# Folded query weights: their seven-product sums made in the fold, and the fold's stores on ScalarE's queue

## The chip, the cores and the metric

The kernel runs on one core of a Trainium2 chip. The core has a matrix engine (TensorE, PE in the profile), a vector engine (VectorE, DVE), an activation engine (ScalarE, ACT), a general engine (GpSimd, POOL) and a synchronisation engine (SyncE, SP). Each takes its own list of instructions in order and waits on semaphores that the others raise. Transfers are issued by SP, POOL or ACT and are carried by 16 DMA engines which all of them share. The metric is the time of one execution in device microseconds. Here the median before the change is 2603.19 us of three runs (2600.45 to 2605.1).

## The reference: what is computed

One layer over 2048 tokens of width 1024, all in float32, with three sub-layers. Each is an RMS norm, a body, an RMS norm of the output and a residual sum.

```python
y = jnp.concatenate([ya, yh], axis=-1) @ w_out       # window attention and gated recurrence, one out projection
h = h + rms_norm(y, g_mix_post)
u = rms_norm(h, g_x_pre);  m = rms_norm(mem, g_mem)
y = cross_attention(u, m, wq_x, wk_x, wv_x, wo_x)     # 4 heads of 256 over 256 memory tokens
h = h + rms_norm(y, g_x_post)
u = rms_norm(h, g_ffn_pre)
y = (silu(u @ w_gate) * (u @ w_up)) @ w_down          # hidden width 2816
h = h + rms_norm(y, g_ffn_post)
```

In cross-attention the memory is short (256 tokens), so the kernel multiplies weights with the memory first. The scores are `u @ QK`, where `QK` (1024 x 1024) is, head by head, the query weight times the keys, with the gain and the scale in it. The output is `p @ VO`, where `VO` (1024 x 1024) is the values times the output weight. Making `QK` and `VO` is called the fold.

## The kernel before

**Number format.** A float32 matrix is split into a high and a low half (`split2`, L893: ACT or POOL makes the high one, DVE the low one), and each product is three TensorE passes (L1032 to L1034: high x high, high x low, low x high).

**Seven products.** The large products from the out projection on are done in a Strassen-Winograd scheme: both operands are cut in two by two blocks and seven block products stand for eight (`seven`, L1036). It needs sums of blocks on both sides. On the streamed side (`streamed`, L974) DVE makes them for each block of 256 rows (L1001). On the side that stays in SBUF (`resident`, L903, tiles `T`) four sums are needed, named by keys 5, 7, 6 and 4 (`CHAIN`, L901). With the four blocks of the matrix called 11, 12 (upper left and right), 21 and 22 (lower), they are 5 = 12 - 11, 7 = 22 - 12, 6 = 7 + 11 and 4 = 21 - 6. They are made ahead of their use and written to a buffer in HBM, from which `resident` loads them.

**Who makes the sums ahead.** `combined` (L936) is a generator that runs beside an earlier stage. For each half of the matrix it loads blocks, waits a few steps, lets DVE subtract or add (L943, placed behind the last traced ACT and DVE instructions by `behind`) and stores the result (L944). In one pass it loads six tiles of 512 KB and stores four, for two halves twelve and eight. `jobs` (L1291) names the stage beside which each set is made: the sums of `QK` (`qk_s`) beside the out projection from its third block on, and those of `VO` (`vo_s`) beside the score product.

**The order of the stages around the change.** The recurrence of the second half of the tokens (`hgrn`, L856) and the fold (`fold_cross`, L277) are interleaved step by step: recurrence and key projection, then the eight 128-column groups of the query weight (L309 to L322), then the value projection, then the four heads of the output weight (L325 to L348). Both the query weight's groups and the output weight's heads end in an ACT eviction from PSUM into a row tile named `x` (three buffers of 512 KB) and a store from there: 128 rows of `QK` to `qk_d` at L321, or 128 rows of `VO` to `vo_d` at L347. All these stores are issued by SP, which also issues every load. After the fold the SBUF pools are closed and those of the streamed stages are opened. The first stage there is the out projection (`mixed_block`, L1400), with `T` from `w_s` and the stream `sraw` from `y_d`. Its evictions add on DVE (L1391). Then the rows are normed and scaled (L1417), the residual is added by a transfer that POOL issues (L1398, `row<-in_x_dram`), the rows are stored and transposed on PE (L1284, evicted at L1285), and the transposed rows are stored for the score product (`score_block`, L1434).

**What sets the order.** Each engine's list is written by a planner that runs over the traced program with its own costs. Within an engine nothing overtakes at run time: an instruction that waits holds all behind it.

Of the kernel before, what the change touches and what calls it, by code (L numbers as in the profile page):

```python
# [11 lines left out]
F32 = mybir.dt.float32  # L12
# [3 lines left out]
ALU = mybir.AluOpType  # L16
AX = mybir.AxisListType

P = 128
T = 2048  # L20
D = 1024
# [3 lines left out]
KT = D // P  # L25
# [4 lines left out]
NT = T // P  # L30
# [6 lines left out]
def f32(ap):  # L37
    return ap.bitcast(F32)
# [10 lines left out]
class Layer:  # L49
# [26 lines left out]

    def store(self, dst, src):
        self.nc.sync.dma_start(dst, src)

    def gain_tile(self):  # L80
        self._n += 1
        return self.gp.tile([P, D], F32, tag="g", name=f"g_{self._n}")
# [46 lines left out]
    def raw_tile(self):  # L129
        self._n += 1  # L130
        return self.wp.tile([P, D], F32, tag="raw", name=f"raw_{self._n}", bufs=3)

    def split_tiles(self):
        self._n += 1
        hi = self.wp.tile([P, D], F32R, tag="hi", name=f"whi_{self._n}", bufs=3)
        lo = self.wp.tile([P, D], F32R, tag="lo", name=f"wlo_{self._n}", bufs=3)
        return hi, lo
# [139 lines left out]
    def fold_cross(self):  # L277

        nc, ph = self.nc, self.xp
        gx = ph.tile([P, KT], F32, name="gx")  # L280
        self.load(gx, self.I["g_x_pre"].rearrange("r (k p) -> p (r k)", p=P))
        nc.vector.tensor_scalar_mul(gx, gx, float(M) ** -0.5)
        g = self.gain(self.I["g_mem"])
        mT = [ph.tile([P, KT, M], F32R, name=f"mT{i}") for i in range(2)]
        raw_tile, split_tiles = self.raw_tile, self.split_tiles

        def projected(w):
            dst = [ph.tile([P, KT, M], F32R, tag=f"kv{i}", name=f"kv{i}_{self._n}") for i in range(2)]
            for j in range(KT):
                wh, wl = self.wcols(w, j, "A")  # L290
                ps = self.bank("sh"[j % 2])[:, :M]
                for part in range(2):
                    if part:
                        yield dst
                    self.mm3(ps, [((wh[:, k, :], wl[:, k, :]), (mT[0][:, k, :], mT[1][:, k, :])) for k in range(KT)],
                             part)
                nc.scalar.activation(dst[0][:, j, :], ps, AF.Copy)
                nc.vector.tensor_tensor(dst[1][:, j, :], ps, f32(dst[0][:, j, :]), ALU.subtract)
                yield dst

        for t in range(M // P):
            m = raw_tile()
            self.load(m, self.I["mem"][t * P:(t + 1) * P, :])
            u = self.pre_norm(m, g)
            self.transpose_split(u, lambda q: mT[0][:, 4 * q:4 * q + 4, t * P:(t + 1) * P],
                                 lambda q: mT[1][:, 4 * q:4 * q + 4, t * P:(t + 1) * P])
        for kT in projected(self.I["wk_x"]):
            yield
        for d in range(KT):  # L309
            th, tl = self.wcols(self.I["wq_x"], d, "A")  # L310
            o = self.io_tile("x")
            for q in range(2):
                ps = self.bank("sh"[q])
                for r in range(2):
                    h = 2 * q + r
                    self.mm3(ps[:, r * M:(r + 1) * M],
                             [((th[:, j, :], tl[:, j, :]), (kT[0][:, j, :], kT[1][:, j, :])) for j in (2 * h, 2 * h + 1)])
                sl = slice(q * 512, (q + 1) * 512)
                nc.scalar.activation(o[:, sl], ps, AF.Copy, scale=gx[:, d:d + 1])
                if q:  # L320
                    self.store(self.qk_d[d * P:(d + 1) * P, :], o)  # L321
                yield  # L322
        for vT in projected(self.I["wv_x"]):
            yield
        for h in range(4):  # L325
            banks = [[self.bank(k) for k in "sh"] for _ in range(2)]
            for i in range(2):
                j = 2 * h + i
                raw = raw_tile()
                self.load(raw, self.I["wo_x"][j * P:(j + 1) * P, :])  # L330
                wh, wl = split_tiles()
                self.split(raw, wh, wl, "A")
                for mt in range(2):
                    ms = slice(mt * P, (mt + 1) * P)
                    ah, al = vT[0][:, j, ms], vT[1][:, j, ms]
                    for q in range(2):
                        sl = slice(q * 512, (q + 1) * 512)
                        nc.tensor.matmul(banks[mt][q], ah, wh[:, sl], start=(i == 0), stop=False)
                        nc.tensor.matmul(banks[mt][q], ah, wl[:, sl], start=False, stop=False)
                        nc.tensor.matmul(banks[mt][q], al, wh[:, sl], start=False, stop=(i == 1))  # L340
                if i == 0:
                    yield
            for mt in range(2):
                o = self.io_tile("x")
                for q in range(2):
                    nc.scalar.activation(o[:, q * 512:(q + 1) * 512], banks[mt][q], AF.Copy)
                self.store(self.vo_d[(2 * h + mt) * P:(2 * h + mt + 1) * P, :], o)  # L347
            yield  # L348


# [585 lines left out]
    def combined(self, get, nk, dst):  # L936

        nc = self.nc
        halves = [(0, (nk + 1) // 2), ((nk + 1) // 2, nk)]
        for a, b in halves:  # L940
            def put(key, t, o, op):
                with self.behind():
                    nc.vector.tensor_tensor(t, t, o, op)  # L943
                self.store(dst[self.CHAIN.index(key), :, a * 512:b * 512], t.rearrange("p k d -> p (k d)"))  # L944

            for x, y, key in (((0, 1), (0, 0), 5), ((1, 1), (0, 1), 7), (None, (0, 0), 6), (None, (1, 0), 4)):
                if x:
                    t = get(0, *x, a, b - a)
                o = get(1, *y, a, b - a)
                for _ in range(3):  # L950
                    yield
                if key == 4:
                    put(4, o, t, ALU.subtract)
                else:
                    put(key, t, o, ALU.add if key == 6 else ALU.subtract)
                yield

    @contextlib.contextmanager
# [117 lines left out]
    def eight(self, S, T, nk, out, addend, halves=False):  # L1076
# [34 lines left out]
        yield  # L1111

    def phases(self, jobs, first, prologue=None):


# [175 lines left out]
    def jobs(self):  # L1291
# [11 lines left out]
        def weights(src, r0, nk):  # L1303
            return lambda t, i, j, k0, n: self.load(
                t, src[r0 + (i * nk + k0) * P:r0 + (i * nk + k0 + n) * P, j * 512:(j + 1) * 512]
                .rearrange("(k p) d -> p k d", p=P))

        def ffn_u(b):
            return lambda t, i, j, k0, n: self.load(
                t, self.u_d[4 * i + k0:4 * i + k0 + n, :, b * TB + j * 512:b * TB + (j + 1) * 512]  # L1310
                .rearrange("k p t -> p k t"))

        def kinds(blocks, first="dd", last="dd"):
            middle = "s" * (len(blocks) - len(first) - len(last))
            return [(k,) + b for k, b in zip(first + middle + last, blocks)]

        def sums(name, src, nk, *tiles):
            dst = self.tc.dram_tile([4, P, nk * 512], F32, name=name)

            def get(which, i, j, k0, n):  # L1320
                t = (tiles or (self.extra_tile, self.gain_tile))[which]().rearrange("p (k d) -> p k d", d=512)[:, :n]
                src(t, i, j, k0, n)
                return t

            return dst, lambda: self.combined(get, nk, dst)

        def in_turn(*what):
            return lambda: itertools.chain.from_iterable(w() for w in what)

        qk, vo = weights(self.qk_d, 0, 4), weights(self.vo_d, 0, 4)  # L1330
        down = [(weights(I["w_down"], f0 * P, nk), f0, nk) for f0, nk in ((0, 3), (6, 4), (14, 4))]
        qk_s, vo_s = sums("qk_s", qk, 4, self.extra_tile, self.row_tile), sums("vo_s", vo, 4)
        u_s = sums("u_s", ffn_u(1), 4)
        x_tile = lambda: self.io_tile("x")
        w_s, self.w_sums = sums("w_s", w_out, 4, x_tile, x_tile)
        self.u_s = self.tc.dram_tile([4, P, 4, 512], F32, name="u_s0")
        d_s = [sums(f"d_s{c}", src, nk) for c, (src, _, nk) in enumerate(down)]
        jobs = [(w_out, 4, kinds([self.mixed_block(n) for n in range(0, NT, 2)]), w_s, {2: [qk_s[1]]}),
                (qk, 4, kinds([self.score_block(n) for n in range(0, NT, 2)]), qk_s[0], {1: [vo_s[1]]}),
                (vo, 4, kinds([self.value_block(n) for n in range(0, NT, 2)]), vo_s[0], {})]  # L1340
        for b in range(NB):
            beside = {2: [in_turn(*(d[1] for d in d_s))]} if b else {4: [u_s[1]]}
# [323 lines left out]
```

## Time and profile before

| | |
|---|---|
| median of three runs | 2603.19 us |
| the profiled execution | 2603.6 us |
| its span, first to last instruction | 2601.7 us |
| mean granted TensorE clock | 0.992 |
| PE / DVE / ACT / POOL busy | 97% / 67% / 49% / 18% |
| moved by DMA | 497.88 MB, mean 191 GB/s |
| recurrence with fold | about 655 to 791 us |
| out projection, and its overlap with the score product | about 797 to 1000 us |

Times in rows are microseconds from the span's start. A row of the timeline has the start, the duration, the engine, the line, the operation with output and inputs, the shape, and in brackets how long the engine had been idle and what ended that. `xN` at the end of a row counts merged instructions; the duration of a merged row runs to the end of its last one. A row of the windows has the stretch, its length, then for PE, weight load (PEld), DVE, ACT and POOL the busy time with the number of instructions, then the granted TensorE clock, the DMA engines' busy share and GB/s. A row by tile has minimum, median and maximum in nanoseconds. `SPq` and the like is an engine's own issue of a transfer.

### The profile page before, as it was taken

To read this page: it belongs to the slowest core of one execution; us is meant where nothing else is said; L and a number is where in the kernel's file an instruction comes from. 1 tells how busy PE (TensorE), PEld (TensorE's weight loads), DVE (VectorE), ACT (ScalarE), POOL (GpSimd) and SP (SyncE) were. 2 spreads that over 40 slices of the span, in tenths; PEclk is the share of its full clock that TensorE was granted. 3 is DMA by queue.
4 is the path that set the end of the run, shared out by engine and by line. 5 is a ranking of instruction groups with operands and counts; after the bars stand their busy time and mean duration, and the time that the engine had idled before them with its cause. 6 is when DMAs were issued, how large, how long until landed. Compare 5 with 4: busy or idle time off the path is not lost.

```text
span 2601.7 us, 34516 instructions
## 1 busy us (share of the span) xinstructions
PE 2528.0 (97%) x12160; PEld 2115.2 (81%) x12160; DVE 1746.0 (67%) x2773; ACT 1262.0 (49%) x2641; POOL 466.6 (18%) x651
## 2 busy tenths in 40 slices
PE   7989999999998999999999999999999999999998
PEld 6878788878997778888778888888888888888786
DVE  7675578887646568786785555576666656664756
ACT  5463366655654565565563333354333335443543
POOL 4240343320312224223320000000000000000022
PEclk9999999999999999999999999999999999999999
DMA  5434655484875998656984532353456434576798
GB/s 186 143 120 167 208 157 171 131 267 157 279 259 207 289 328 258 221 191 187 302 273 138 167 124 73 105 186 116 167 182 230 147 108 168 174 225 174 232 228 208
DMA packets 286350, 497.88 MB, mean 191 GB/s; under 512 B 20576, under 2 KB 143456, under 8 KB 286176
## 3 DMA queue, kind: packets, MB, share of 16 engines
q1 hardware_dynamic: 275520, 456.87, 52.3%
q0 software_dynamic: 10656, 38.80, 8.0%
q8 instruction: 96, 1.57, 0.2%
q14 instruction: 78, 0.64, 0.1%
HBM read 328.87 MB, written 166.72 MB: 190 GB/s over the span
## 4 chain that ended last, share of the span: by engine, by line
PE 80%; DMA 8%; DVE 4%; issue 3%; POOL 2%; ACT 2%; SPq 0%; DVEq 0%; POOLq 0%; ACTq 0%
PE psm L1032 22%; PE psm L1034 22%; PE psm L1033 22%; PE psg L163 2%; PE psg L164 2%; PE psg L165 2%; DMA row<-in_x_dram 1%; PE pss L1284 1%; DMA row<-h_d 1%; DMA u_d<-row 1%; DMA h_d<-row 1%; DMA x<-in_w_out_dram 1%; ACT junk L1369 1%; DMA pair<-in_x_dram 1%; DMA extra<-qk_d 0%
## 5 line engine op out<-in xcount | busy, mean ns | idle before, releaser
L1032 PE MATMUL psm<-T,S 128*128 128x512 f32 x2664 | 1036.4, 393 | 24.6 <-ACT S L896 13.8
L1033 PE MATMUL psm<-T,S 128*128 128x512 f32 x2664 | 1041.9, 391 | 0.0
L1034 PE MATMUL psm<-T,S 128*128 128x512 f32 x2664 | 1037.3, 392 | 2.6 <-DVE S L899 2.5
L1032 PEld LDWEIGHTS psm<-T,S 128*128 128x128 f32 x2664 | 503.3, 189 | 132.6 <-ACT S L896 15.1
L1034 PEld LDWEIGHTS psm<-T,S 128*128 128x128 f32 x2664 | 502.5, 189 | 109.2 <-DVE S L899 4.8
L1033 PEld LDWEIGHTS psm<-T,S 128*128 128x128 f32 x2664 | 503.2, 189 | 103.3
L896 ACT ACTIVATE S<-sum 128x512 fp32r<-128x512 f32 (+1 forms) x338 | 208.0, 619 | 340.1 <-PE psm L1034 331.7
L899 DVE TENSOR_TENSOR S<-sraw,S 128x512 fp32r<-128x512 f32 (+1 forms) x311 | 214.4, 697 | 224.4 <-ACT S L896 214.9
L899 DVE TENSOR_TENSOR S<-sum,S 128x512 fp32r<-128x512 f32 (+1 forms) x404 | 277.1, 690 | 84.3 <-ACT S L896 66.6
L1047 ACT ACTIVATE part<-psm 128x512 f32<-128x512 f32 x297 | 175.1, 592 | 174.9 <-PE psm L1034 168.0
L896 ACT ACTIVATE S<-sraw 128x512 fp32r<-128x512 f32 (+1 forms) x272 | 166.8, 617 | 154.7 <-PE psm L1034 143.1
L1398 POOL DMA_DIRECT2D row<-y_d x28 | 25.0, 892 | 1131.4 <-DMA sraw<-hid_d 964.8
L1369 ACT ACTIVATE junk<-row 128x512 f32<-128x512 f32 x160 | 99.7, 624 | 121.8 <-DVE row L1391 33.4
L899 DVE TENSOR_TENSOR T<-row,T 128x1024 fp32r<-128x1024 f32 x104 | 123.0, 1190 | 28.7 <-ACT T L896 28.5
L163 PE MATMUL psg<-u,whi 128*128 128x512 f32 x352 | 141.2, 401 | 1.0 <-POOL whi L145 1.0
L165 PE MATMUL psg<-u,wlo 128*128 128x512 f32 x352 | 139.5, 396 | 1.5 <-DVE wlo L146 1.5
L164 PE MATMUL psg<-u,whi 128*128 128x512 f32 x352 | 139.6, 397 | 0.0
L896 ACT ACTIVATE T<-row 128x1024 fp32r<-128x1024 f32 x104 | 105.8, 1027 | 23.7 <-DMA row<-in_w_down_dram 10.9
L146 DVE TENSOR_TENSOR wlo<-raw,whi 128x1024 fp32r<-128x1024 f32 x54 | 68.8, 1275 | 33.2 <-ACT whi L143 26.6
L898 POOL TENSOR_SCALAR S<-sum 128x512 fp32r<-128x512 f32 x66 | 49.0, 742 | 234.7 <-PE psm L1034 141.0
L1550 DVE TENSOR_TENSOR part<-psm,part 128x512 f32<-128x512 f32 x66 | 45.4, 688 | 64.6 <-PE psm L1034 64.5
L1541 DVE TENSOR_TENSOR row<-psm,part 128x512 f32<-128x512 f32 x66 | 45.5, 689 | 57.4 <-PE psm L1034 57.3
(329 smaller groups left out, 3644.3 us busy)
## 6 DMA issues: line engine op xcount, KB each, us to landing
sraw<-in_w_gate_dram SPq DMA_DIRECT2D x44, 512.0 KB, 4.9
sraw<-in_w_up_dram SPq DMA_DIRECT2D x44, 512.0 KB, 4.8
hid_d<-row SPq DMA_DIRECT2D x44, 512.0 KB, 2.7
h_d<-row SPq DMA_DIRECT2D x32, 512.0 KB, 6.9
y_d<-row SPq DMA_DIRECT2D x32, 512.0 KB, 3.6
sraw<-hid_d SPq DMA_DIRECT2D x32, 512.0 KB, 5.2
row<-h_d POOLq DMA_DIRECT2D x30, 512.0 KB, 8.1
row<-y_d POOLq DMA_DIRECT2D x28, 512.0 KB, 7.3
```

The lines of the kernel that those rows point to most:

```text
L146: nc.vector.tensor_tensor(lo, raw, f32(hi), ALU.subtract)
L163: nc.tensor.matmul(ps, ah, bh, start=(i == 0), stop=False)
L164: nc.tensor.matmul(ps, ah, bl, start=False, stop=False)
L165: nc.tensor.matmul(ps, al, bh, start=False, stop=(i == n - 1))
L896: self.nc.scalar.activation(hi, raw, AF.Copy)
L898: self.nc.gpsimd.tensor_scalar(hi, raw, 1.0, 1.0, ALU.mult, ALU.mult)
L899: self.nc.vector.tensor_tensor(lo, raw, f32(hi), ALU.subtract)
L1032: nc.tensor.matmul(ps, s[:, 0, k, :], t[:, 0, k, :], start=st, stop=False, **kw)
L1033: nc.tensor.matmul(ps, s[:, 0, k, :], t[:, 1, k, :], start=False, stop=False, **kw)
L1034: nc.tensor.matmul(ps, s[:, 1, k, :], t[:, 0, k, :], start=False, stop=sp, **kw)
L1047: nc.scalar.activation(t, ps, AF.Copy)
L1369: self.nc.scalar.activation(junk, a, AF.Square, scale=float(D) ** -0.5, accum_out=to)
```

## The change

Three things change.

1. The column groups of the query weight are taken in the order 0, 4, 1, 5, 2, 6, 3, 7. The row tile of an upper group (0 to 3) is kept until that of the lower group four further on is there. From the two, DVE makes the four sums of `CHAIN` for these rows: `a` is 5 (left) and 7 (right), `b` is 6 (left) and 4 (right). Two row tiles `qs` of 512 KB are added for them. SP stores the four halves of 256 KB each to `qk_s`, for four pairs of groups: 16 sums of 128x512 and 16 stores.
2. The pass of `combined` over `QK` beside the out projection is gone, with its twelve loads, eight sums of 128x1024 and eight stores. `qk_s` is now a buffer that only the fold writes.
3. The fold's 16 stores of `x` rows, eight to `qk_d` and eight to `vo_d`, are issued by ACT instead of SP.

```diff
+    def put(self, dst, src):
+        self.nc.scalar.dma_start(dst, src)
...
-        for d in range(KT):
+        upper = None
+        for d in (0, 4, 1, 5, 2, 6, 3, 7):
             th, tl = self.wcols(self.I["wq_x"], d, "A")
             o = self.io_tile("x")
...
                 nc.scalar.activation(o[:, sl], ps, AF.Copy, scale=gx[:, d:d + 1])
                 if q:
-                    self.store(self.qk_d[d * P:(d + 1) * P, :], o)
+                    self.put(self.qk_d[d * P:(d + 1) * P, :], o)
                 yield
+            if d < 4:
+                upper = o
+                continue
+            a, b = [ph.tile([P, D], F32, tag="qs", name=f"qs{d}_{i}", bufs=2) for i in range(2)]
+            l, r = slice(0, 512), slice(512, D)
+            nc.vector.tensor_tensor(a[:, l], upper[:, r], upper[:, l], ALU.subtract)
+            nc.vector.tensor_tensor(a[:, r], o[:, r], upper[:, r], ALU.subtract)
+            nc.vector.tensor_tensor(b[:, l], a[:, r], upper[:, l], ALU.add)
+            nc.vector.tensor_tensor(b[:, r], o[:, l], b[:, l], ALU.subtract)
+            for c, t in enumerate((a[:, l], a[:, r], b[:, l], b[:, r])):
+                self.store(self.qk_s[c, :, (d - 4) * 512:(d - 3) * 512], t)
...
-                self.store(self.vo_d[(2 * h + mt) * P:(2 * h + mt + 1) * P, :], o)
+                self.put(self.vo_d[(2 * h + mt) * P:(2 * h + mt + 1) * P, :], o)
...
-        qk_s, vo_s = sums("qk_s", qk, 4, self.extra_tile, self.row_tile), sums("vo_s", vo, 4)
+        self.qk_s = self.tc.dram_tile([4, P, 4 * 512], F32, name="qk_s")
+        vo_s = sums("vo_s", vo, 4)
...
-        jobs = [(w_out, 4, kinds([self.mixed_block(n) for n in range(0, NT, 2)]), w_s, {2: [qk_s[1]]}),
-                (qk, 4, kinds([self.score_block(n) for n in range(0, NT, 2)]), qk_s[0], {1: [vo_s[1]]}),
+        jobs = [(w_out, 4, kinds([self.mixed_block(n) for n in range(0, NT, 2)]), w_s, {}),
+                (qk, 4, kinds([self.score_block(n) for n in range(0, NT, 2)]), self.qk_s, {1: [vo_s[1]]}),
```

The helper inside `combined` is renamed from `put` to `made`, since `put` is now a method; it does the same.

More of the change, by code (lines that the diff above doesn't have):

```diff
@@ L940, in combined, with made @@
         for a, b in halves:
-            def put(key, t, o, op):
+            def made(key, t, o, op):
                 with self.behind():
@@ L952, in combined @@
                 if key == 4:
-                    put(4, o, t, ALU.subtract)
+                    made(4, o, t, ALU.subtract)
                 else:
-                    put(key, t, o, ALU.add if key == 6 else ALU.subtract)
+                    made(key, t, o, ALU.add if key == 6 else ALU.subtract)
                 yield
```

## The prediction

> **What bounds the kernel now.** I read the page's busy shares and chain first, then the engine windows, then what TensorE (PE) waited for between 640 and 1000 us, where all edited code runs, and last the timelines around each of those waits. Lines 1 and 2 are of the page; then waits as total, times, longest; then windows.
>
> ```profile
> PE 2528.0 (97%) x12160; PEld 2115.2 (81%) x12160; DVE 1746.0 (67%) x2773; ACT 1262.0 (49%) x2641; POOL 466.6 (18%) x651
> PE 80%; DMA 8%; DVE 4%; issue 3%; POOL 2%; ACT 2%; SPq 0%; DVEq 0%; POOLq 0%; ACTq 0%
> ...
> PE psm L1032 <- ACT S L896: 6.9, 1, 6.9
> PE pss L1284 <- DMA row<-in_x_dram: 5.3, 2, 2.9
> PE pss L1284 <- ACT row L1285: 2.3, 2, 2.0
> PE psm L1032 <- DVE row L1391: 1.4, 1, 1.4
> PE psm L1032 <- ACT part L1047: 0.8, 1, 0.8
> ...
> 690.00:760.00 70.00, 68.65 (x580) 68.30 (x579) 34.05 (x46) 39.98 (x104) 23.20 (x27) 1.00 0.81 268
> 760.00:790.00 30.00, 30.00 (x165) 25.69 (x164) 12.37 (x13) 17.00 (x27) 0.00 (x0) 1.00 0.66 232
> 850.00:950.00 100.00, 92.19 (x425) 75.41 (x424) 56.57 (x73) 50.93 (x125) 30.27 (x53) 0.97 0.95 297
> 1000.00:1100.00 100.00, 100.00 (x483) 83.21 (x482) 80.04 (x148) 57.46 (x147) 27.12 (x37) 0.99 0.72 240
> ```
>
> PE is busy 97% of the span, so no edit beside it pays unless it touches one of PE's few gaps. The change removes no matmul. Three stretches matter: the fold (690 to 790: PE full, DMA 0.81 then 0.66), the out projection (850 to 950: PE loses 7.8 us while DMA is at 0.95) and, to compare, the score stage (PE full at DMA 0.72).
>
> **Part 1, the fold's stores leave SP's queue.** The timeline at the border between fold and out projection:
>
> ```profile
> 775.46 1.77 SPq L75 DMA_DIRECT2D raw<-in_wo_x_dram  x2
> 790.18 0.39 PE L340 MATMUL psh<-whi,kv 128*128 128x512 f32 x1
> 790.37 0.32 SPq L78 DMA_DIRECT2D vo_d<-x  x1
> 790.71 0.62 ACT L346 ACTIVATE x<-psh 128x512 f32<-128x512 f32 x1
> 790.78 1.25 SPq L75 DMA_DIRECT2D sraw<-y_d  x2
> 796.82 0.63 ACT L896 ACTIVATE S<-sraw 128x512 fp32r<-128x512 f32 x1 [5.50 <-DMA sraw<-y_d]
> 797.50 0.79 PE L1032 MATMUL psm<-T,S 128*128 128x512 f32 x1 [6.94 <-ACT S L896]
> ...
> 757.51 0.75 DVE L852 SCALAR_TENSOR_TENSOR sg<-psg,onorm,sg 128x512 f32<-128x512 f32 x1 [1.34 <-DMA sg<-z_d]
> ...
> 798.00:800.00 2.00, 2.00 (x6) 1.47 (x5) 0.87 (x2) 0.63 (x1) 0.00 (x0) 0.50 1.05 410
> 800.00:802.00 2.00, 2.00 (x8) 1.57 (x7) 1.25 (x2) 0.63 (x1) 0.47 (x1) 0.72 1.05 406
> ```
>
> The first stream load (`sraw<-y_d`) is issued at 790.78 because SP takes its queue in order and a `vo_d` store, which waits for ACT's eviction, stands ahead of it until 790.37. Its data come 6.0 us later, after PE has run dry at 790.57. The memory it fills was the recurrence's, whose last DVE instruction starts at 757.51, so nothing else holds it. With the stores on ACT's queue SP is done with the fold at 777.2 and the load can land before 785. Next in line is then ACT: its last eviction ends at 791.33, the cast takes 0.63, PE starts at about 792.0. The gap falls from 6.94 to 1.4: -5.5. PE also restarted at half clock (0.50, then 0.72: half until 801.1), 3.6 us at half is 1.8 lost; after a gap of 1.39 us (below, at 910) I take none. Sum -7.3. Ends: 0 (the loads come as late as now) and -8.7 (no gap left).
>
> ACT now issues 16 stores. No row shows ACT issuing one: below, SP needs 0.33 for such a store, POOL 0.89 for its kind. I take SP's, the same sort of plain transfer: 16 x 0.33 = 5.3 us of ACT, up to 14.3. ACT is idle 30.0 of 70 us in the first stretch and 13.0 of 30 in the second, so the price is 0; uncovered it would be those 5.3. A gain below zero is excluded for ACT's own time. What queues behind a store on ACT is the next weight cast (L143) and eviction. SP loses 16 stores and gets 16 others.
>
> **Part 2, no sums beside the out projection.** The loads, sums and stores around the three largest gaps of 850 to 950:
>
> ```profile
> 869.17 1.23 DVE L943 TENSOR_TENSOR extra<-extra,row 128x1024 f32<-128x1024 f32 x1 [3.52 <-DMA row<-qk_d]
> 871.51 2.47 DVE L1417 SCALAR_TENSOR_TENSOR row<-row,q_r,g 128x1024 f32<-128x1024 f32 x2
> 873.09 0.94 POOL L1398 DMA_DIRECT2D row<-in_x_dram  x1 [4.51 <-DVE row L1417]
> 882.40 1.34 PE L1284 MATMUL pss<-ident,row 128*128 128x128 f32 x8 [2.40 <-DMA row<-in_x_dram]
> 908.23 1.23 DVE L943 TENSOR_TENSOR extra<-extra,row 128x1024 f32<-128x1024 f32 x1 [5.51 <-DMA extra<-qk_d]
> 910.21 0.47 PE L1032 MATMUL psm<-T,S 128*128 128x512 f32 x1 [1.39 <-DVE row L1391]
> 919.34 0.95 POOL L1398 DMA_DIRECT2D row<-in_x_dram  x1 [1.68 <-DVE row L1417]
> 930.10 1.26 PE L1284 MATMUL pss<-ident,row 128*128 128x128 f32 x8 [2.94 <-DMA row<-in_x_dram]
> ...
> 884.00:886.00 2.00, 2.00 (x6) 1.61 (x5) 0.69 (x1) 1.28 (x4) 0.46 (x1) 0.50 1.02 353
> 886.00:888.00 2.00, 2.00 (x9) 1.57 (x9) 1.81 (x3) 1.50 (x6) 1.10 (x3) 0.89 1.02 418
> 932.00:934.00 2.00, 2.00 (x6) 1.60 (x5) 2.00 (x4) 1.10 (x4) 0.00 (x0) 0.50 0.58 232
> ```
>
> The edit takes out 12 loads and 8 stores of 512 KB (10.5 MB) and 8 sums at 1.2 us. The gap of 882 begins with the sum: DVE sits 3.52 us at L943 for a sum's load, so the scaling (L1417) and POOL's adding transfer are late. That of 910 is the same wait, 5.51 long, with the eviction L1391 behind it. That of 930 is the adding transfer itself, 10.8 us from issue to use while DMA is full. Of the 29.7 MB that 850 to 950 moves (297 GB/s) up to 10.5 go, which brings the DMA share to 0.95 x 19.2 / 29.7 = 0.61, below the 0.72 at which the score stage runs PE full. So I take all four gaps: 2.40 + 1.39 + 2.94 + 0.8 = 7.5. After 882 and 930 PE ran 3.4 us at half clock (the 0.50 rows and their neighbours), 1.7 lost each. Sum -10.9. Ends: -5.5 (882 with its clock and 910 only, where the removed wait itself is the cause) and -14.6 (also the 2.0 gap at 999 with 1.7 of clock, which hangs on a store under a full DMA). The freed DVE and SP time is worth nothing more.
>
> [...]
>
> **Part 3, sums in the fold.** Added are 16 sums of 128x512 and 16 stores of 256 KB (4.2 MB). Rows for their prices, from the fold's transfers and the groups by tile:
>
> ```profile
> q1 hardware_dynamic: 14935, 18.62, 80.7%
> qk_d<-x SPq DMA_DIRECT2D x8, 512.0 KB, 5.2
> L78 SPq DMA_DIRECT2D qk_d<-x x8: 319/332/506, 704.9 to 745.7; - x8
> L1398 POOL DMA_DIRECT2D row<-y_d x28 | 25.0, 892 | 1131.4 <-DMA sraw<-hid_d 964.8
> L1001 DVE TENSOR_TENSOR sum<-sraw,sraw x4: 678/693/954, 800.8 to 823.4; 128x512 f32<-128x512 f32 x4
> 719.24 0.69 DVE L823 TENSOR_TENSOR W<-psg,W 128x512 f32<-128x512 f32 x1 [2.88 <-PE psg L821]
> 735.76 0.69 DVE L843 TENSOR_TENSOR on<-pst,h_rs 128x512 f32<-128x512 f32 x1 [2.87 <-POOL h_rs L842]
> ```
>
> DVE: 16 x 0.69 = 11.1 us, beside 36 us of idle DVE in 690 to 760. Each pair is a chain of 2.8 us waiting for ACT's second eviction; behind it stand the next low halves (L146) and the recurrence. DVE has holes of 2.9 us just there, so 0; uncovered, 2.8 per pair or 11.1. SP: 16 x 0.33 = 5.3 us of issue, each behind a sum, ahead of weight and recurrence loads. DMA: 80.7% of 70 us for 18.62 MB is 3.03 us per MB, so 4.2 MB need 12.7 us of all engines; 13.3 are free in 690 to 760, but the stores fall in its last 45 us, where about 8.6 are free. 4.1 us are over and delay loads: +4.1. Ends: 0 (the rest spills past 760, where 10.2 are free) and +12.7 (all on the path). The new order of columns and the longer life of `x` rows cost nothing by themselves: a row is freed one column later, and columns are 5.8 us apart (8 stores from 704.9 to 745.7) against a 2.8 us chain.
>
> **Sum.** -7.3 - 10.9 + 4.1 = -14.1. The profiled execution took 2603.6 us (span 2601.7), the median is 2603.19, so nearly the same. 2603.6 - 14.1 = 2589.5 is the forecast.
>
> **Rivals.** *The border stays (R1).* The loads are late for another reason, such as transfers that share the same engines. For it: DMA reads 1.05 at 798. Against: DMA is at 0.66 before 790 and SP's wait is plain. Only part 1 drops: 2603.6 - 10.9 + 4.1 = 2596.8. [...]
>
> *The fold pays in full (R2).* DMA is the bound there: +12.7, and the stores it delays take half of part 1: 2603.6 - 3.7 - 10.9 + 12.7 = 2601.7, no change. For it: 0.81 and a PE that has used 68.65 of 70 us. Against: nobody waits soon for these stores.
>
> *ACT is held by its own stores (R3, slower).* If a store on ACT blocks it until an earlier transfer lands (5.2 us median), 8 x 5.2 = 41.6 us fall into the 46 us of the query columns, where ACT is idle 43%, 19.8 us. PE starves for the other 21.8: 2589.5 + 21.8 = 2611.3. It decides from 2.5 us of blocking per store. Against: SP's store rows last 0.33. For: nothing has shown ACT storing.
>
> **Chances.** Forecast 0.53, R1 0.14, R2 0.17, R3 0.16. About 0.2% (5.2 us) is what a measurement can tell. Forecast and R1 are faster (0.67), R2 is within (0.17), R3 slower (0.16). Range: from parts 1 and 2 at -7.3 and -14.6 with a free fold, 2582, to beyond R2, 2605; R3 is left out, with the tail of the best case. The forecast's own range is 2582 to 2598.
>
> **What would show it.** Right: `sraw<-y_d` issued before 785 and a gap under 2 us at the border, with the clock kept; no L943 before the score stage, DMA share below 0.72 and PE full in the out projection; PE idle in the fold up by a few us at most. Wrong: ACT idle behind its store rows, PE waiting for `whi` or `wlo` in the fold, or the border's gap still near 7.

## The result and the profile after

The changed kernel takes 2592.48 us in the median (2588.79 to 2600.14), the kernel before, measured beside it, 2603.83 us. The ratio is 0.9958 (95% interval 0.9951 to 0.9964): about 11 us faster, where 14.1 were forecast. The profiled execution has a span of 2590.1 us against 2601.7. Between the two sources the lines shift: L1032 to L1034 of before are L1047 to L1049 after, L896 is L911, L899 is L914, L943 is L958, L1284 and L1285 are L1299 and L1300, L1398 is L1414, L346 is L361. ACT's new stores are L81.

First what PE waited for between 640 and 1000 us after the change (total, times, longest):

```profile
PE pss L1299 <- ACT row L1300: 2.8, 2, 2.2
PE psm L1049 <- DVE S L914: 2.3, 1, 2.3
PE pss L353 <- ACT x L361: 2.0, 1, 2.0
PE psm L1047 <- ACT S L911: 1.8, 1, 1.8
```

The 6.9 us at the border are 1.8 now. The 5.3 us on the adding transfer, the 1.4 on an eviction and the 0.8 on a `part` are gone. Two waits are new, 2.3 us for a low half of `S` and 2.0 us for a row `x` in the fold.

The windows of the same kernel (stretch, length, busy PE, PEld, DVE, ACT, POOL, clock, DMA share, GB/s):

```profile
690.00:760.00 70.00, 69.25 (x584) 68.88 (x584) 43.85 (x64) 40.91 (x106) 23.25 (x27) 1.00 0.95 325
850.00:950.00 100.00, 99.33 (x479) 81.81 (x478) 60.74 (x78) 60.24 (x140) 32.66 (x54) 1.00 0.81 243
950.00:1000.00 50.00, 45.51 (x196) 36.90 (x195) 37.72 (x47) 32.14 (x68) 20.17 (x27) 0.90 0.91 282
```

PE is full in the out projection at full clock, with the DMA engines at 0.81. In the fold they are at 0.95 and PE hardly notices. The third row is where time is lost: PE 45.5 of 50 us, and the clock at 0.90.

Where the time went is best seen by comparing the start of the k-th matmul of one profile with that of the other, since both have 12160. Both kernels order some matmuls of neighbouring stages differently, so single values can be off by about a microsecond. Negative is earlier than before, in us. Each row is one profiled execution, that of `queue_only` and of `more_stores` the shortest of their ten and that of `traffic` the longest, so gains in time are taken from the medians:

```
reached before at (us)            704.8   759.7   786.7   841.0   935.8  1064.6
stage that ends there           recurr. columns val./wo  border out pr.   score
after                              -0.1    -0.9    +1.3    -5.0   -17.0   -10.3
sums_only                          -0.2    -1.9    -0.5    +0.0   -12.0    -7.6
queue_only                         +0.3    -0.5    +0.4    -4.5    -8.1    -7.1
late_vo                            +0.4    -1.4    -0.7    -7.0   -19.2   -19.2
late_vo_u                          -0.9    -2.6    -2.6    -9.2   -21.3   -21.8
u_rows                             +2.5    +1.7    +1.7    -3.3   -15.2   -11.3
traffic                            -0.4    -1.8    +0.7    -3.3    -6.4    -1.4
traffic_lag                        +1.0    -0.4    +1.7    -3.1   -13.2    -5.0
more_stores                        +1.8   +10.1   +11.4    +8.1    -3.1    -0.7
volume_only                        +1.4   +19.6   +31.1   +27.8   +16.3   +22.2
```

The other rows belong to the experiments below. For the change itself: the border gives 6.3 us (from +1.3 to -5.0) and the out projection 12.0. Then 6.7 are lost again where the out projection meets the score product.

The border, from the timeline of after:

```profile
777.23 18.21 SPq L75 DMA_DIRECT2D sraw<-y_d  x6
786.79 0.60 ACT L361 ACTIVATE x<-pss 128x512 f32<-128x512 f32 x1 [4.43 <-DMA vo_d<-x]
787.43 0.50 PE L353 MATMUL pss<-whi,kv 128*128 128x512 f32 x1 [1.98 <-ACT x L361]
791.91 0.33 ACTq L81 DMA_DIRECT2D vo_d<-x  x1
793.96 0.50 PE L1047 MATMUL psm<-T,S 128*128 128x512 f32 x1 [1.82 <-ACT S L911]
```

The stream loads begin at 777.23 and not at 790.78, since no store that waits for an eviction stands ahead of them on SP. The gap is 1.82 us. An ACT store takes 0.33 us of ACT. What ACT did wait for is a row buffer: 4.43 us until an earlier `vo_d` store had landed, and 1.98 of that reached PE.

The out projection's transfers in 850 to 950 (out, in, engine, count, size, median us to landing):

```profile
DMA packets 8371, 24.35 MB, mean 243 GB/s; under 512 B 752, under 2 KB 752, under 8 KB 8364
...
row<-in_x_dram POOLq DMA_DIRECT2D x8, 512.0 KB, 7.2
sraw<-h1t_d SPq DMA_DIRECT2D x5, 512.0 KB, 6.3
...
row<-qk_s SPq DMA_DIRECT2D x4, 512.0 KB, 7.7
```

The adding transfer in the same view of the kernel before:

```profile
row<-in_x_dram POOLq DMA_DIRECT2D x8, 512.0 KB, 10.4
```

The stretch moves 24.35 MB instead of 29.7. The score product's own loads (`sraw<-h1t_d`, `row<-qk_s`) have moved up into the room, so the share is 0.81 and not 0.61. The adding transfer lands after 7.2 us and not after 10.4.

The place where time is lost again, from the timeline and the windows of after:

```profile
978.29 1.38 SPq L75 DMA_DIRECT2D g<-vo_d  x1
981.01 4.17 SPq L78 DMA_DIRECT2D h_d<-row  x2
...
983.97 1.50 PE L1299 MATMUL pss<-ident,row 128*128 128x128 f32 x8 [2.23 <-ACT row L1300]
986.97 1.23 DVE L958 TENSOR_TENSOR extra<-extra,g 128x1024 f32<-128x1024 f32 x1 [3.21 <-DMA g<-vo_d]
988.71 0.68 DVE L914 TENSOR_TENSOR S<-sum,S 128x512 fp32r<-128x512 f32 x1
989.45 0.80 PE L1049 MATMUL psm<-T,S 128*128 128x512 f32 x1 [2.27 <-DVE S L914]
...
986.00:988.00 2.00, 1.18 (x3) 0.36 (x2) 1.03 (x1) 2.00 (x8) 1.52 (x4) 0.50 1.03 419
992.00:994.00 2.00, 2.00 (x6) 1.54 (x6) 1.96 (x4) 0.44 (x1) 0.00 (x0) 0.50 0.65 131
994.00:996.00 2.00, 2.00 (x9) 1.60 (x8) 1.29 (x2) 0.00 (x0) 0.62 (x1) 0.79 0.77 246
```

It is the mechanism that the prediction described for the removed pass, now on the other pass of `combined`, the one over `VO`. Its load (`g<-vo_d`) is issued between stores of `h_d` and lands late. DVE sits 3.21 us at the sum L958, and the low half of `S` behind it comes late by as much. PE has gaps of 2.23 and 2.27 us within 8 us, and the clock is at half from 984.6 to 994.8 (0.65, four rows of 0.50 and 0.79 in the windows from 984 to 996). Of the two gaps only the second hangs on the sum. The kernel before has the first one too, and it has the same wait of DVE, but no second gap:

```profile
999.00 1.92 PE L1284 MATMUL pss<-ident,row 128*128 128x128 f32 x8 [2.02 <-ACT row L1285]
999.95 1.22 DVE L943 TENSOR_TENSOR extra<-extra,g 128x1024 f32<-128x1024 f32 x1 [3.20 <-DMA g<-vo_d]
```

There the sum starts 0.95 us after PE has gone on, here 3.00 us after. The second gap costs 2.27 us, and the clock is at half for 10.2 us where it was for 3.4 in the kernel before (0.77, 0.50 and 0.87 in the windows from 998 to 1004). In these 10.2 us PE works 8.0, with a matmul every 0.43 us, and every 0.23 from 995 on. Taken as half, the loss is 4.0 us, where it was 1.7 before. So by estimate about 4.5 of the 6.7 us come with the second gap; for the rest no cause is shown.

### The profile page after: what moved, and what is told of

Its sections match the earlier page's. It is cut to its first block, busy times and chain, and to the rows that moved or that the text cites. A ratio compares the mean times of both kernels' runs of the same rounds, so it can differ in the third digit from the quotient of the medians.

```text
span 2590.1 us, 34500 instructions
## 1 busy us (share of the span) xinstructions
PE 2525.1 (97%) x12160; PEld 2113.1 (82%) x12160; DVE 1749.0 (68%) x2781; ACT 1260.9 (49%) x2641; POOL 470.5 (18%) x651
## 4 chain that ended last, share of the span: by engine, by line
PE 78%; DMA 9%; DVE 4%; issue 4%; POOL 3%; ACT 2%; SPq 0%; POOLq 0%; DVEq 0%; ACTq 0%
PE psm L1047 21%; PE psm L1049 21%; PE psm L1048 21%; PE psg L168 2%; PE psg L166 2%; PE psg L167 2%; PE pss L1299 1%; DMA row<-h_d 1%; DMA row<-in_x_dram 1%; DVE S L914 1%; DMA row<-d_s 1%; DMA kk<-z_d 1%; DMA x<-in_w_out_dram 1%; DMA g<-u_d 1%; DMA sraw<-in_w_in_dram 1%
## 5 line engine op out<-in xcount | busy, mean ns | idle before, releaser
L1047 PE MATMUL psm<-T,S 128*128 128x512 f32 x2664 | 1035.8, 393 | 18.2 <-ACT S L911 9.5
L1049 PE MATMUL psm<-T,S 128*128 128x512 f32 x2664 | 1038.0, 392 | 4.1 <-DVE S L914 3.9
L1047 PEld LDWEIGHTS psm<-T,S 128*128 128x128 f32 x2664 | 502.9, 189 | 126.3 <-ACT S L911 11.1
L1049 PEld LDWEIGHTS psm<-T,S 128*128 128x128 f32 x2664 | 502.3, 189 | 110.9 <-DVE S L914 7.3
L911 ACT ACTIVATE S<-sum 128x512 fp32r<-128x512 f32 (+1 forms) x338 | 207.9, 619 | 336.6 <-PE psm L1049 328.1
L914 DVE TENSOR_TENSOR S<-sraw,S 128x512 fp32r<-128x512 f32 (+1 forms) x311 | 214.0, 696 | 216.5 <-ACT S L911 205.6
L914 DVE TENSOR_TENSOR S<-sum,S 128x512 fp32r<-128x512 f32 (+1 forms) x404 | 277.1, 690 | 87.7 <-ACT S L911 68.5
L911 ACT ACTIVATE S<-sraw 128x512 fp32r<-128x512 f32 (+1 forms) x272 | 166.6, 617 | 147.9 <-PE psm L1049 144.6
L1414 POOL DMA_DIRECT2D row<-y_d x28 | 25.0, 892 | 1130.3 <-DMA sraw<-hid_d 964.4
L914 DVE TENSOR_TENSOR T<-row,T 128x1024 fp32r<-128x1024 f32 x104 | 123.6, 1196 | 30.8 <-ACT T L911 30.4
L911 ACT ACTIVATE T<-row 128x1024 fp32r<-128x1024 f32 x104 | 105.7, 1027 | 23.2 <-DMA row<-in_w_down_dram 9.3
L1566 DVE TENSOR_TENSOR part<-psm,part 128x512 f32<-128x512 f32 x66 | 45.5, 689 | 64.9 <-PE psm L1049 64.9
L149 DVE TENSOR_TENSOR wlo<-raw,whi 128x1024 fp32r<-128x1024 f32 x54 | 68.0, 1260 | 27.0 <-ACT whi L146 19.8
L1557 DVE TENSOR_TENSOR row<-psm,part 128x512 f32<-128x512 f32 x66 | 45.5, 690 | 57.6 <-PE psm L1049 57.4
```

Source lines behind the costliest of these rows:

```text
L149: nc.vector.tensor_tensor(lo, raw, f32(hi), ALU.subtract)
L911: self.nc.scalar.activation(hi, raw, AF.Copy)
L914: self.nc.vector.tensor_tensor(lo, raw, f32(hi), ALU.subtract)
L1047: nc.tensor.matmul(ps, s[:, 0, k, :], t[:, 0, k, :], start=st, stop=False, **kw)
L1049: nc.tensor.matmul(ps, s[:, 1, k, :], t[:, 0, k, :], start=False, stop=sp, **kw)
```

## The experiments

Ratios are to the kernel before, with 95% intervals. Four kernels add transfers to a buffer that nobody reads (`traffic`, `traffic_lag`, `more_stores`, `volume_only`); all of them still compute the whole layer.

**One part at a time.** `sums_only` is the changed kernel with the fold's stores back on SP:

```diff
     def put(self, dst, src):
-        self.nc.scalar.dma_start(dst, src)
+        self.nc.sync.dma_start(dst, src)
```

> The sums are made in the fold, but all the fold's stores stay on SP's queue. If the two gains are separate (my reading), the border between fold and out projection shows its gap of about 7 us and its half clock again, the out projection stays without gaps: 6 us slower than the changed kernel, about 2598. If the out projection's gain needed the early start that the queue gives, the gaps at the added residual come back too and the time is about 2603. If the fold suffers from SP waiting for evictions while it also has the sums' stores, slower than 2603.

`queue_only` is the kernel before with only the queue changed:

```diff
-                    self.store(self.qk_d[d * P:(d + 1) * P, :], o)
+                    self.put(self.qk_d[d * P:(d + 1) * P, :], o)
...
-                self.store(self.vo_d[(2 * h + mt) * P:(2 * h + mt + 1) * P, :], o)
+                self.put(self.vo_d[(2 * h + mt) * P:(2 * h + mt + 1) * P, :], o)
```

> The kernel before with the fold's 16 stores on ACT's queue and the sums beside the out projection as they were. My reading: the border's gap falls from 6.9 to under 2 us and keeps its clock, the out projection keeps its gaps at 2.4, 1.4 and 2.9 us with the sums' waits: 6 to 7 us faster than before, about 2597. If issuing from another queue saves nothing but the initiation, 2603.5. If ACT is held up by its own stores, slower than 2604.

Measured: `sums_only` 2596.75 us, 0.9973 (0.9962 to 0.9983); `queue_only` 2599.73 us, 0.9982 (0.9973 to 0.9992). What PE waited for between 690 and 1010, first `sums_only`, then `queue_only` (whose L1035 and L1287 are L1032 and L1284 of before):

```profile
PE psm L1047 <- ACT S L911: 7.7, 2, 6.9
PE psm L1049 <- DVE S L914: 3.6, 1, 3.6
```

```profile
PE pss L1287 <- DMA row<-in_x_dram: 4.5, 2, 2.4
PE psm L1035 <- ACT S L899: 2.5, 2, 1.8
```

With the stores on SP the 6.9 us at the border are back, with everything else of the change in place. With the queue alone they go, and the waits on the adding transfer stay. The parts give 7.0 and 4.7 us, together 11.7 against 11 for both: two separate gains that add up. One thing came otherwise than expected for `queue_only`: its clock was not kept at the border, but is 0.95 in the mean of 790 to 826 us in this profile (1.00 in the changed kernel), by estimate 3 to 4 us at half.

**Which stores matter.** `vo_queue` is the changed kernel with the eight `qk_d` stores back on SP:

```diff
-                    self.put(self.qk_d[d * P:(d + 1) * P, :], o)
+                    self.store(self.qk_d[d * P:(d + 1) * P, :], o)
```

> The changed kernel with the query rows' stores (qk_d) back on SP and only the value rows' stores (vo_d) on ACT. My reading: only the latter stand ahead of the first stream loads, so the time is that of the changed kernel within 2 us, 2590.5 to 2594.5. If the query rows' stores mattered in the fold (SP waiting for evictions ahead of loads while DMA is full), PE idles in 700 to 760 and it is 3 us or more slower.

2592.15 us, 0.9954 (0.9937 to 0.9971): no difference from the changed kernel that can be seen. So the stores that count are those of `vo_d`, the last of which stand ahead of the stream loads.

**The loss where the stages meet.** `late_vo` moves the pass over `VO` one place later in the score product:

```diff
-                (qk, 4, kinds([self.score_block(n) for n in range(0, NT, 2)]), self.qk_s, {1: [vo_s[1]]}),
+                (qk, 4, kinds([self.score_block(n) for n in range(0, NT, 2)]), self.qk_s, {2: [vo_s[1]]}),
```

> The changed kernel with the sums of VO begun one pair of blocks later beside the score product (its third block instead of its second). In the changed kernel PE loses about 6 us where out projection and score product meet (gaps of 2.2 and 2.3 us and 10 us at half clock), which the kernel before lost less of. If the first sum of VO, for whose load DVE waits 3.2 us there, causes it, the gap at the low half of S goes and 3 to 6 us are gained, 2587 to 2590. If the full DMA with the loads of T and the residual's transfers causes it, nothing changes, within 1.5 us of the changed kernel.

`before_late` is the same edit on the kernel before.

> The kernel before with nothing changed but the sums of VO begun one pair of blocks later beside the score product. If the loss where out projection and score product meet was there before and only of another size, 2 to 4 us faster, about 2600. If the change brought it, as its earlier tail meets the loads of T, no difference, 2603.5.

`late_vo` 2586.01 us, 0.9932 (0.9916 to 0.9949); `before_late` 2605.11 us, 1.0003 (0.9992 to 1.0014). PE's waits of `late_vo` and its window where the stages meet:

```profile
PE pss L1299 <- ACT row L1300: 1.9, 1, 1.9
PE psm L1047 <- ACT S L911: 1.8, 1, 1.8
PE pss L353 <- ACT x L361: 0.4, 1, 0.4
...
950.00:1000.00 50.00, 48.01 (x220) 39.34 (x219) 41.77 (x57) 34.71 (x79) 19.13 (x31) 0.97 0.88 278
```

The wait of 2.3 us for `S` is gone and PE does 2.5 us more in that stretch, at 0.97 clock instead of 0.90. In the table the 19.2 us stay 19.2 through the score product. The difference from the changed kernel is 0.0026 of 2603.8, 6.8 us (2.2 to 11.4, the two intervals combined). On the kernel before the same edit brings nothing that can be seen. There the pass over `VO` delayed nobody: the gap at this place was the one of 2.02 us, for another wait, which `late_vo` keeps with 1.9. `late_vo` leaves the pass's first load where it was (974.10, again between stores of `h_d`) and moves its first sum to 1003.62, so what counts is the sum's place in DVE's list and not the load's in SP's. The wait for the low half of `S` (2.8 to 3.7 us) is also in six of the seven other kernels that are built on the change and leave the pass in its place (all but `volume_only`), and in none of the three that move it. So the loss belongs to the new situation, and by the middle of its interval it hides over a third of what the change is worth.

**Was it the bytes or the sums?** `traffic` puts the old pass's 12 loads and 8 stores back beside the out projection, without DVE's sums:

```diff
+    def moved(self, get, nk, dst):
...
+                    t = get(0, *x, a, b - a)
+                o = get(1, *y, a, b - a)
+                for _ in range(3):
+                    yield
+                s = o if key == 4 else t
+                self.store(dst[self.CHAIN.index(key), :, a * 512:b * 512], s.rearrange("p k d -> p (k d)"))
...
-        jobs = [(w_out, 4, kinds([self.mixed_block(n) for n in range(0, NT, 2)]), w_s, {}),
+        jobs = [(w_out, 4, kinds([self.mixed_block(n) for n in range(0, NT, 2)]), w_s, {2: [spare[1]]}),
```

> The changed kernel, and beside the out projection the old pass's 12 loads and 8 stores run again into a buffer that nobody reads, without the 8 sums on DVE: 10.5 MB of transfers come back, DVE's waits for them do not. If the volume makes the out projection's gaps (full DMA, the adding transfer late), most of its gain of about 12 us is lost, about 2602. If DVE's waits for the sums' loads make them, the gain stays, within 3 us of 2592. My reading of the rows: the gaps at 882 and 910 hung on DVE's waits (5.5 us with the clock), that at 930 on the volume (4.6 us), so about 2597.

2601.02 us, 0.9987 (0.9978 to 0.9996). That is 0.0029 above the changed kernel, 7.5 us (4.7 to 10.4): most of what both parts had won is lost again, with no sum on DVE. Its largest gap:

```profile
857.34 1.08 ACT L1314 ACTIVATE row<-pss 128x512 f32<-128x512 f32 x2 [6.00 <-DMA h_d<-row]
...
857.99 1.33 PE L1313 MATMUL pss<-ident,row 128*128 128x128 f32 x5 [4.87 <-ACT row L1314]
...
849.63 0.37 SPq L75 DMA_DIRECT2D extra<-vo_d  x1
850.10 1.77 SPq L78 DMA_DIRECT2D h_d<-row  x2
...
SPq L75 <- DMA spare<-extra: 17.3, 4, 8.2
```

A row buffer is not free because its store to `h_d` is late. On SP that store stood behind a load into `extra` (849.63), and this load waited 8.2 us until a `spare` store out of that buffer had landed (the last row is of SP's waits between 797 and 1000 us). So the transfers, with the waits for their buffers, suffice; DVE's wait at a sum, on which the prediction put two of the four gaps, is not needed for a loss of this size. It does not follow that DVE's waits cost nothing in the kernel before: the gaps lie elsewhere here.

`traffic_lag` was to separate the bytes from SP's waits: each store sends the row loaded one step earlier.

```diff
-                s = o if key == 4 else t
-                self.store(dst[self.CHAIN.index(key), :, a * 512:b * 512], s.rearrange("p k d -> p (k d)"))
+                for to, s in late:
+                    self.store(to, s.rearrange("p k d -> p (k d)"))
+                late = [(dst[self.CHAIN.index(key), :, a * 512:b * 512], o)]
```

> Beside the out projection the 12 loads and 8 stores of the old pass run again as in the run that moved the data without sums, but each store sends the row tile that was loaded one step earlier, into a buffer that nobody reads, so that SP need not wait for a load it has just issued. All of the reference is computed. Theory V (the old pass cost its volume on the DMA engines): as slow as the run with the stores right behind their loads, 2599 to 2602 us, 0.998 of before, adding transfer still near 9 us, DMA share of 850 to 950 above 0.85. Theory Q (the old pass cost SP's waits for its own loads, which held the loads and stores of the stage behind them): SP's waits for the transfers of the extra buffer, 44 us in 797 to 1000 there, fall below 15 us, and the time falls to 2592 to 2596 us.

2598.36 us, 0.9976 (0.9967 to 0.9986). SP's waits between 797 and 1000 us and the window of the out projection:

```profile
SPq L78 <- DMA row<-qk_d: 30.4, 7, 7.0
...
SPq L75 <- DMA extra<-qk_d: 14.1, 4, 5.2
...
850.00:950.00 100.00, 95.46 (x453) 77.33 (x452) 55.26 (x73) 56.07 (x133) 31.42 (x56) 1.00 0.96 309
```

The edit did not do what it was for: SP still waits 44.5 us for the pass's own loads. The time lies between the two theories, and its distance to `traffic` (0.0011, 2.9 us, -0.6 to 6.3) is not resolved. So the 12 loads and 8 stores alone cost 7.5 us in the one run and 4.7 us (1.7 to 7.7) in the other; how that divides between full DMA engines and a blocked SP queue is open.

`volume_only` was to add bytes with no wait at all, as 20 copies of 512 KB from one HBM buffer to another:

```diff
+                for c in range(k):
+                    n = next(at)
+                    self.load(dst[n], src[(n % 8) * P:(n % 8 + 1) * P, :])
+                    yield
```

> The changed kernel, with 20 copies of 512 KB from HBM to HBM beside the out projection into a buffer that nobody reads, in the steps where the old pass had its 12 loads and 8 stores: the same 10.5 MB through the DMA engines, but no SBUF tile, nothing that SP has to wait for and no work on DVE. If the volume is what made the out projection slow, as slow as with the old loads and stores, about 2601. If it was SP's queue, where loads and stores of the pass waited for tiles and held up the stream's loads and the rows' stores, near the changed kernel, 2592 to 2595.

2624.8 us, 1.0073 (1.0059 to 1.0086). It missed its place: nothing of the out projection holds the copies back, and SP issued them as soon as `qk_d` was there. All copies by destination and source, then the first window of the fold:

```profile
L75 SPq DMA_DIRECT2D spare<-qk_d x20: 467/474/819, 713.2 to 778.0; - x20
...
690.00:760.00 70.00, 63.07 (x497) 61.60 (x496) 34.41 (x49) 33.66 (x90) 22.94 (x27) 0.96 0.97 348
```

They ran in the fold, and there the table grows by 29.7 us (from +1.4 to +31.1), against 1.4 in the changed kernel. So it says nothing on the out projection, but it does say what the fold bears.

**How much room the fold has.** `more_stores` issues every store of a sum twice:

```diff
                 self.store(self.qk_s[c, :, (d - 4) * 512:(d - 3) * 512], t)
+                self.store(self.spare[c, :, (d - 4) * 512:(d - 3) * 512], t)
```

> The changed kernel with each of the fold's 16 sum stores issued twice, the second into a buffer that nobody reads: 4.2 MB more in a stretch where DMA is already at 0.95. If the spilling stores cost PE nothing but a late row buffer (as the 2 us gap at an eviction near 787 shows), 1 to 4 us slower, 2593 to 2597. If DMA is the bound there now, 12.7 us slower, 2605.

2607.87 us, 1.0004 (0.9993 to 1.0016). Against the changed kernel that is 0.0046, 12.0 us (8.5 to 15.5), for 4.2 MB more. Its first window of the fold:

```profile
690.00:760.00 70.00, 65.34 (x535) 64.72 (x533) 38.72 (x56) 35.46 (x92) 23.81 (x27) 0.98 0.97 326
```

The DMA share only goes from 0.95 to 0.97, and PE loses 4 us in this stretch. The last 45 us of it, in which the stores fall, say more. They are shown for the kernel before, the changed kernel and `more_stores`:

```profile
715.00:760.00 45.00, 43.65 (x370) 43.30 (x369) 22.20 (x30) 24.84 (x66) 12.61 (x15) 1.00 0.80 267
715.00:760.00 45.00, 45.00 (x384) 45.00 (x383) 30.86 (x43) 27.47 (x69) 12.42 (x15) 1.00 1.00 353
715.00:760.00 45.00, 40.34 (x325) 39.72 (x323) 24.98 (x36) 22.25 (x56) 11.13 (x13) 0.96 1.03 354
```

The change fills these 45 us, from 267 to 353 GB/s, and `more_stores` moves no more in them (354). The first 4.2 MB cost at most 1.4 us, the second the whole of the gain by the medians. The ten times of `more_stores` spread from 2599.94 to 2609.49 us, and its profile, of the shortest, has 8.2 us in the fold for the second 4.2 MB (9.6 in the table, less the 1.4).

**The row buffer in the fold.** `u_rows` lets the rows of `VO` alternate between two sets of buffers:

```diff
-                o = self.io_tile("x")
+                o = self.io_tile("xu"[mt])
```

> The changed kernel with the value rows taken in turn from two kinds of row buffers, and the sums of VO where the change has them. If the late row buffer is all that the fold pays, its gap of 2.0 us goes and 1 to 3 us are gained, about 2590; what then is lost where out projection and score product meet, stays.

2591.65 us, 0.9944 (0.9929 to 0.996), not resolved from the changed kernel. The profile shows the gap of 1.98 us gone:

```profile
794.04 0.50 PE L1047 MATMUL psm<-T,S 128*128 128x512 f32 x1 [1.82 <-ACT S L911]
...
760.00:790.00 30.00, 30.00 (x172) 26.02 (x171) 14.29 (x17) 16.69 (x25) 0.00 (x0) 1.00 0.82 286
...
796.00:798.00 2.00, 2.00 (x6) 1.61 (x5) 2.00 (x3) 0.00 (x0) 0.99 (x1) 0.50 0.99 392
```

The first row is of PE's timeline, the others are windows. PE is full to the end of the fold, where the changed kernel lost its 1.98 us. The first and the last row are the border's gap and the clock behind it, which come up below.

**A better version.** `late_vo_u` has both edits, of `late_vo` and `u_rows`.

> The changed kernel with the sums of VO one pair of blocks later, and the value rows taken in turn from two kinds of row buffers (three and two) instead of three of one kind. If ACT's wait for a store to free a row (4.4 us, PE's gap of 2.0) is what the fold pays, 1 to 2 us faster than with the later sums alone, 2584 to 2585; if something else, no difference from 2586.

2582.86 us, 0.9919 (0.9898 to 0.9941), the fastest of all, 21 us under the kernel before; its distance to `late_vo` alone is not resolved. `best` stores, on top of that, only the left half of the upper rows of `QK`, 1 MB less:

```diff
-                    self.put(self.qk_d[d * P:(d + 1) * P, :], o)
+                    n = 512 if d < 4 else D
+                    self.put(self.qk_d[d * P:(d + 1) * P, :n], o[:, :n])
```

> The later sums of VO and the two kinds of row buffers, and for the upper four column groups only the left half of each row is stored to qk_d, since the right half (block 12) is read only in the sums: 1 MB less in the fold. With DMA at 0.95 there and 4.2 MB more costing 15 us, 1 MB less should give 0 to 2 us below 2583; it can't cost anything.

2588.61 us, 0.9937 (0.9923 to 0.995). Saving 1 MB in the fold gains nothing that can be seen. The median is 4.7 us above that of `late_vo_u` (-1.9 to 11.3 by the ratios), which is not resolved, and the times spread from 2584.79 to 2594.95.

## Why the prediction was right, and where it was not

**The sum.** Forecast -14.1 us, measured about -11. By the table the terms are -6.3 (part 1, forecast -7.3), -12.0 (part 2, -10.9) and +1.4 (part 3, +4.1), in sum -16.9 by 936 us. The rest is a loss of 6.7 us that no step named, partly made up by another 1 us in later stages. That the total still came within 3 us is in part luck: part 3 had been charged 2.7 us too much, part 2 credited 1.1 too little and part 1 credited 1.0 too much, which together made up for 2.8 of the 6.7.

**Part 1 was right, in its place and its cause.** The loads are issued at 777.23, as worked out; the gap is 1.82 us, under the 2 that were named; the clock stays full in this profile (1.00 in 790 to 826). The clock was luck: nine profiles have this gap of 1.8 us at the border, and the clock of 790 to 826 is 1.00 in five of them, 0.98 in `traffic`, 0.97 in `traffic_lag` and 0.95 in `queue_only` and `u_rows`, where by estimate 3 to 4 us ran at half and about 1.7 were lost. `sums_only` brings the wait back and `queue_only` takes it away alone, for 4.7 us (2.1 to 7.0). The term was 1 us too large. R1 falls. So does the first of the two alternatives put down for `queue_only`, no gain at 2603.5: it took 2599.73. What was saved is a wait of 13.6 us at the head of SP's queue (790.78 less 777.23).

**Part 1's price for ACT was in the wrong item.** The stores take ACT 0.33 us each, and ACT is not held by issuing them; R3 falls. But the text counted as queued behind a store only the next cast and eviction. It left out that a row buffer comes free only when its store has landed, and that ACT itself then waits in the eviction: 4.43 us once, 1.98 of it on PE. This is R3's mechanism in small, by way of the buffer. It is most of the +2.2 us between 759.7 and 786.7 in the table. `u_rows` and `late_vo_u`, with more row buffers, have none there, so it comes with the buffers. Its size varies: the same fold shows a wait of 0.4 us in `late_vo`. What part the sums' stores have in it is not settled: `queue_only`, without them, has +0.9 there, and `sums_only`, with the stores on SP, has +1.4 with a wait of 1.1 us for another thing, a low half of a weight (L149).

**Part 2 had its size and its effect, but its cause only in part.** All four gaps went, the half clock with them (0.97 in 850 to 950 before, 1.00 after), and no sum of `combined` runs beside the out projection (the next is at 986.97). Two conditions failed. The DMA share was to fall below 0.72 and is 0.81, since the next stage's loads moved into the room; PE is full all the same, so 0.72 was no limit but only the share of a stage in which PE happened to be full. And the lower end of -5.5 took DVE's wait at L943 as the cause of two gaps; `traffic` gives back 7.5 us with no sum there, though by gaps at other places.

**Part 3 had the room right and the price too high.** Columns and sums cost PE nothing (-0.9 at the end of the columns). The stores did fall into the last 45 us, and the share there rose from 0.80 to 1.00, which is 9.0 us of all engines where about 8.6 had been said to be free. But these 45 us moved 3.9 MB more (353 against 267 GB/s): 2.3 us per MB, where 3.03 had been taken. So nearly all of the 4.2 MB fitted and the 4.1 us over were not there; the +1.4 that remains is mostly the row buffer. R2's price of 12.7 us for 4.2 MB is close to what the second 4.2 MB cost by the medians, 12.0 us. R2 named the right mechanism and was one such load short of it.

**What was missed.** The prediction looked at every wait of the removed pass and at none of the pass that stays. It ended part 2 with the freed DVE and SP time being worth nothing more, and did not ask what the sums of the next pass, the one over `VO`, would hold up. DVE waited 3.2 us for the load of its first sum in the kernel before as well, without a gap of PE behind it. In the changed kernel that wait falls 2 us later against PE's work (3.00 us after PE has gone on, and not 0.95), and the low half of `S` behind it comes too late. Why it falls later is not shown. That the sum's place is the cause is shown by `late_vo`, which moves the pass's sums later and gains 6.8 us, and by `before_late`, which does the same where they were not in the way and gains nothing.

## What to carry to other kernels

A load that prefetches for the next stage belongs on a queue in which no store waits for the last evictions of this one: here a store with 0.32 us of issue held the first stream loads until 790.78, where they otherwise go out at 777.23, and taking the fold's stores off that queue gained 4.7 us by itself. When work is taken out beside one stage, look at what that stage's speed brings forward: here the first sum of the next background pass then stood in the way and cost 6.8 of the 17 us, until it was moved by one place. In this fold, at a DMA share of 0.81, 4.2 MB more cost at most 1.4 us and the next 4.2 MB 2 to 3 us for each MB. The share over the 70 us hardly shows the difference (0.95 and 0.97); the rate does, which rose from 268 to 325 GB/s with the first and only to 326 with the second.

## What the runs showed of the hardware

**The same gap may cost the clock or not.** The gap of 1.82 us at the border kept the clock in the changed kernel and cost 3.4 us at half speed in `u_rows` (0.89, 0.50 and 0.76 in the windows from 794 to 800), with the same work around it. After keeps 1.00 there:

```profile
794.00:796.00 2.00, 2.00 (x8) 1.36 (x9) 2.00 (x4) 0.95 (x2) 0.07 (x1) 1.00 1.05 416
796.00:798.00 2.00, 2.00 (x10) 1.64 (x9) 2.00 (x4) 0.00 (x0) 1.23 (x2) 1.00 1.02 415
```

Other gaps of 1.4 to 2.9 us went either way too. In before the clock stayed at 1.00 after that of 1.39 us at 910 and fell to 0.50 after those of 2.40, 2.94 and 2.02 us (at 882, 930 and 999). In after it stayed at 1.00 after that of 1.98 us at 787 and was at 0.50 from 984.6 to 994.8 around those of 2.23 and 2.27 us. What decides it is not shown. For a sum like the prediction's, a gap near 2 us was worth its length plus 0 or, by estimate from 3.4 us at half clock, 1.7 us.

**This fold's DMA price is steep once the engines are full (share 1.00 in 715 to 760).** Copying 10.5 MB from HBM to HBM during the fold cost 28.3 us more than the changed kernel's fold in the table (29.7 less 1.4; 2.7 us per MB). Storing 4.2 MB more from SBUF cost 8.2 us there (9.6 less 1.4; 2.0 us per MB) and 12.0 us by the medians (2.9 us per MB). The first 4.2 MB had cost at most 1.4, the wait for the row buffer included.
